# Two gate columns instead of one behind the mixer's last transposes, and one behind its last scan's end

## The chip, the cores and the metric

The kernel runs on one core of one Trainium2 chip. The metric is the device time of one execution in microseconds: a median of 3093.51 us over three runs (3091.14 to 3101.21). TensorE (PE) does the matmuls, VectorE (DVE) and ScalarE (ACT) the elementwise work, and SyncE (SP), ScalarE and GpSimd (POOL) each have a queue from which they issue transfers. Each engine works off its own instructions in the order in which they were built into the program; a wait at the head holds up all that is behind it.

## The reference

A trunk of two layers over 528 tokens (16 learned ones and 512) of width 1024. Each layer is a half-step SwiGLU block, a mixer and another half-step block, each followed by a layer norm of the scaled input plus the block's output. The mixer is what the change touches:

```python
z = x @ w_in
glu_a, glu_b, zr, gate_c, gate_r = split(z)
yc = conv_branch(glu_a, glu_b, ...)      # 31-tap depthwise convolution, layer norm, @ conv_wo
yr = rwkv_branch(zr, ...)                # per head: a state S (64 x 64), stepped through the tokens:
#   S = S * w_t + (S @ -kk_t) (kk_t * a_t)^T + v_t k_t^T ;  y_t = S @ r_t
#   y = group norm of y over each head, + bonus, * g, then @ rwkv_wo
h = sigmoid(gate_c) * yc + sigmoid(gate_r) * yr
return h @ w_out
```

Everything is float32; a product is formed from three matmuls on parts, `hi*xh + hi*xl + lo*xh`, so each weight is split into a high and a low part.

## The kernel before

**The mixer's stages.** A mixer projects the input (the columns of `w_in`, 128 output channels each), runs four scans, each for a quarter of the heads, and then joins the branches. A *column* is one such projection: 8 slices of the input, 3 products and 2 halves of the tokens, 48 matmuls of 264 tokens (L229). 32 columns per layer, 16 for the convolution's gated input and 16 for the two gates, depend on no scan. They are kept in a list, `fill`, and handed out at chosen places by `filler(n)`: so many between the chunks of each scan (`FILL`), so many at each seam between two scans (`FILLS`). They are the last in the list that this change concerns: all of them are gate columns. Such a column is evacuated by a tanh on ScalarE (L1045) and written to memory by ScalarE's queue (L1047).

**A scan.** It goes through 8 chunks of 64 tokens. A chunk is a chain over engines: v transposed (L1349), products with the state (L1354), a copy on ScalarE (L1356), two interleaved product groups (L1363, L1366), a copy (L1369), products that give the output and the state's step (L1371), and two operations on VectorE that make the next state (L1376, L1377). The matmuls of the columns stand in between.

**The end of a mixer.** After a scan its outputs are group normed on VectorE (L1408 to L1429), transposed (L1470), scaled (L1472 on ScalarE), given the bonus and the gate (L1474, L1475 on VectorE) and written to `yscr` (L1476; in the last scan by POOL's queue). The last scan's first half is treated during its second half; its second half after its end. The join then reads `yscr` back (L1537, POOL), casts it to a high part (`rh`, L105) and a low part (`rl`, L106), and multiplies by `rwkv_wo` (L210). The convolution's result is read from `cscr` (L1549, SP) for its layer norm.

**What sets the order.** The program is written out by a scheduler that orders each engine's instructions by the order of the code and by when their inputs are expected, so a column whose weights are there may be placed earlier than where the code calls for it, and some L229 matmuls of one column stand apart from the rest. `nosync(later, earlier)` adds an order that the scheduler must keep, with no wait on the chip. `self.later` uses it: the next column's first matmul is kept behind the named instruction. `self.turned` is the last transpose (L1470).

**A column's weights.** SP loads the raw weights (two buffers). For gate columns ScalarE casts the high part in two halves (L140), writes the negated raw into the low part (L146), and a transfer on POOL's queue adds (L147). The high and low parts have two buffers each, so a column's parts can be made only when the column two before it is finished. The first two columns of `rwkv_wo` use the same buffers, in one cast (L142) and a subtraction on VectorE (L153).

Of the kernel before, what the change touches and what calls it, by code (L numbers as in the profile page):

```python
# [70 lines left out]

FILL0 = (0, 0, 0, 0, 2, 0, 0, 0, 2)
FILL = ((0, 0, 0, 0, 0, 0, 0, 0), (0, 0, 0, 0, 0, 0, 0, 0), (0, 0, 0, 0, 0, 0, 0, 0), (0, 1, 0, 1, 0, 1, 0, 0))
FILLS = (3, 3, 4, 2)
FILLP = ((0, 0, 0, 0, 0, 0), (0, 0, 0, 0, 0, 2), (0, 0, 0, 0, 0, 1), (0, 0, 0, 0, 0, 0))
LAST = 1
SCORES = (2, 1, 1, 1, 1, 1, 1, 1)


# [12 lines left out]
class Trunk:  # L92
# [645 lines left out]
    def mixer(self, l, last, pre, more):  # L738
# [48 lines left out]
        def filler(n):  # L787
            for _ in range(min(n, len(fill))):
                fill.pop(0)()
# [3 lines left out]
        def prep(q):  # L793
            Q = {}
            for i, _ in enumerate(self.prep(q, Q)):
                filler(FILLP[q][i])
                self.taps(TAPP[q])
            return Q
# [14 lines left out]
        for q in range(4):  # L813
# [27 lines left out]
            post = early or self.post(q, Q)  # L841
            filler(FILLS[q])
            Q, N = N, prep(q + 2) if q < 2 else None
        for _ in post:
            pass
        filler(len(fill) - LAST)
        self.later = self.turned
        filler(len(fill))
# [485 lines left out]
    def scan(self, q, Q):  # L1334


        nc, mp = self.nc, self.mp
        G, SB, pc, sv = Q["G"], self.sb, Q["pc"], Q["sv"]
        hc = lambda x: x.rearrange("p (h v) -> p h v", h=4)
        ysb = mp.tile([P, NCH * 4, 32], F32, name="b4", bufs=B4)  # L1340
        ysb = ysb.rearrange("p a b -> p (a b)").rearrange("p (m h v) -> p m h v", m=4, h=4)
        Q["y"] = ysb
        for c in range(NCH):
            cs = slice(NM + c * C, NM + (c + 1) * C)
            left = lambda h: slice(h * HS, (h + 1) * HS)
            right = lambda h: slice(256 + h * HS, 256 + (h + 1) * HS)
            tr = self.sm("tr")
            for p in range(2):
                nc.tensor.transpose(tr[0:C, p * P:(p + 1) * P], Q["v"][p][:, cs], self.ident)  # L1349
            nc.scalar.copy(sv[0:C], hc(tr[0:C, 0:256]))  # L1350
            va, w = (mp.tile([P, 4, HS], F32, name=x, bufs=n) for x, n in (("va", 2), ("w0", W0)))
            nc.scalar.copy(va[0:C], hc(tr[0:C, 0:256]))
            for h in range(4):
                nc.tensor.matmul(tr[0:C, right(h)], G[:, h // 2, h % 2, 0, cs], sv[:, h, :],  # L1354
                                 start=True, stop=True)
            nc.scalar.copy(w[0:C], hc(tr[0:C, 256:512]))  # L1356


            ch = self.sm("ch")
            chain = []  # L1360
            rows = slice(0, P if c + 1 < NCH else C)
            for h in range(4):
                chain.append(nc.tensor.matmul(ch[C:P, left(h)], G[0:C, h // 2, h % 2, 1, cs],  # L1363
                                              w[0:C, h, :], start=h == 0, stop=True,
                                              skip_group_check=True))
                chain.append(nc.tensor.matmul(ch[0:C, right(h)], G[HS:P, h // 2, h % 2, 1, cs],  # L1366
                                              sv[HS:P, h, :], start=h == 0, stop=False,
                                              skip_group_check=True))
            nc.scalar.copy(va[C:P], hc(ch[C:P, 0:256]))  # L1369
            for h in range(4):  # L1370
                chain.append(nc.tensor.matmul(ch[rows, right(h)], SB[:, c, h, rows], va[:, h, :],  # L1371
                                              start=False, stop=True, skip_group_check=True))
            nsv = None
            if c + 1 < NCH:
                nsv = self.new_state()
                nc.vector.tensor_tensor(nsv[HS:P], hc(ch[HS:P, 256:512]), sv[HS:P], op=ALU.add)  # L1376
                nc.vector.tensor_tensor(nsv[HS:P], nsv[HS:P],  # L1377
                                        pc[HS:P, :, c + 1:c + 2].to_broadcast([HS, 4, HS]),
                                        op=ALU.mult)
            for later, earlier in zip(chain[1:], chain):  # L1380
                self.nosync(later, earlier)
            ro = C * (c % 2)
            nc.scalar.copy(ysb[ro:ro + C, c // 2], hc(ch[0:C, 256:512]))
            sv = nsv
            yield
# [305 lines left out]
```

## Time and profile before

| | |
|---|---|
| median of three runs | 3093.51 us (3091.14 to 3101.21) |
| the profiled execution's own time | 3093.63 us, span 3091.9 us |
| TensorE busy | 2972.3 us, 96% of the span |
| VectorE, ScalarE, GpSimd busy | 2278.3, 1436.2, 178.3 us |
| chain that ended last, by engine | TensorE 82%, VectorE 7%, DMA 5%, ScalarE 3% |
| column matmuls (L229) | 5280, about 300 ns each as shown |
| end of the last scan to the join's first product, layer 0 | 1020.72 to 1041.12 us |
| the same, layer 1 | 2544.09 to 2563.67 us |

A matmul's duration as shown overlaps the next one's, so the pace is read from starts, not from durations. The clock that TensorE was granted is given per stretch as a share of its full speed; it is 1.00 or 0.50 at any moment. Idle time stands in brackets in front of the instruction that waited, with what released it. Line numbers are those of the kernel before; in the changed kernel lines after 845 are one higher, and after 1382 two higher.

### The profile page before, as it was taken

How to read it: one execution, taken by the hardware profiler on the slowest of the kernel's cores; microseconds unless marked ns; L12 is line 12 of the kernel's file. 1: busy time of each engine (PE TensorE's matmuls, PEld its weight loads, DVE VectorE, ACT ScalarE, POOL GpSimd, SP SyncE). 2: the span in 40 equal slices, each digit the busy share in tenths (PEclk: the TensorE clock that was granted, in tenths of full speed). 3: DMA queues.
4: the chain of work that ended last, by engine and by line, in shares of the span. 5: the costliest groups of instructions: out<-in, count | busy, mean ns of one | idle time of the engine just before them, and what ended most of it. 6: DMA issues, size and time to landing. Idle time of an engine off the chain costs nothing.

```text
span 3091.9 us, 63773 instructions
## 1 busy us (share of the span) xinstructions
PE 2972.3 (96%) x25908; PEld 2860.6 (93%) x25908; DVE 2278.3 (74%) x4687; ACT 1436.2 (46%) x2551; POOL 178.3 (6%) x286
## 2 busy tenths in 40 slices
PE   8999989999999899999999999899999989999997
PEld 7999989889888899999989999899899879999997
DVE  5676777888876678666786767778888857687767
ACT  4454454344454544444454444543444545254443
POOL 0010000000000000010000000000000000001100
PEclk9999999999999899999999999999899999999998
DMA  6565534335355654565545654344354655546651
GB/s 180 145 148 130 127 108 153 98 86 133 100 125 130 181 147 125 134 149 139 133 121 130 154 130 120 129 147 101 81 127 111 151 129 166 156 121 146 152 139 62
DMA packets 555699, 405.25 MB, mean 131 GB/s; under 512 B 89292, under 2 KB 500288, under 8 KB 555406
## 3 DMA queue, kind: packets, MB, share of 16 engines
q1 hardware_dynamic: 519854, 308.49, 34.8%
q0 software_dynamic: 30944, 84.18, 14.7%
q10 hardware_dynamic: 4608, 8.52, 0.8%
q8 instruction: 203, 3.33, 0.5%
q14 instruction: 90, 0.74, 0.1%
HBM read 270.81 MB, written 47.12 MB: 103 GB/s over the span
## 4 chain that ended last, share of the span: by engine, by line
PE 82%; DVE 7%; DMA 5%; ACT 3%; issue 2%; SPq 1%; ACTq 0%; DVEq 0%; POOLq 0%
PE mm L210 53%; PE mm L229 16%; PE sc L1285 2%; PE ch L1371 2%; PE tr L1354 1%; PE sc L1204 1%; PE ch L1363 1%; DMA w_raw<-in_ffn_wu_dram 1%; DMA w_raw<-in_w_in_dram 1%; DVE cacc L1033 1%; DVE w_lo L153 1%; ACT w_hi L142 1%; PE sc L957 1%; DVE ln_rstd L403 1%; PE sc L1089 1%
## 5 line engine op out<-in xcount | busy, mean ns | idle before, releaser
L210 PE MATMUL mm<-xh,w_hi 128*128 128x264 f32 (+1 forms) x1792 | 515.4, 289 | 20.8 <-ACT xh L417 14.7
L210 PE MATMUL mm<-xh,w_lo 128*128 128x264 f32 (+1 forms) x1792 | 513.9, 287 | 0.5 <-DVE w_lo L153 0.5
L210 PE MATMUL mm<-xl,w_hi 128*128 128x264 f32 (+1 forms) x1792 | 513.8, 287 | 0.5 <-DVE xl L418 0.3
L210 PE MATMUL mm<-hh,w_hi 128*128 128x264 f32 (+1 forms) x1408 | 399.5, 284 | 2.0 <-ACT hh L105 2.0
L210 PE MATMUL mm<-hl,w_hi 128*128 128x264 f32 (+1 forms) x1408 | 399.4, 284 | 0.5 <-DVE hl L106 0.4
L210 PE MATMUL mm<-hh,w_lo 128*128 128x264 f32 (+1 forms) x1408 | 399.7, 284 | 0.0
L229 PE MATMUL mm<-xh,w_lo 128*128 128x264 f32 x1760 | 392.3, 300 | 7.3 <-DMA w_lo<-w_raw 7.0
L229 PE MATMUL mm<-xh,w_hi 128*128 128x264 f32 x1760 | 388.1, 298 | 6.2 <-DVE kp L907 2.9
L229 PE MATMUL mm<-xl,w_hi 128*128 128x264 f32 x1760 | 387.4, 297 | 0.0
L210 PEld LDWEIGHTS mm<-xh,w_hi 128*128 128x128 f32 x1792 | 342.7, 192 | 23.9 <-ACT xh L417 16.6
L1033 DVE SCALAR_TENSOR_TENSOR cacc<-cu,cw,cacc 128x528 f32<-128x528 f32 (+1 forms) x480 | 356.0, 753 | 4.4 <-ACT cacc L1031 0.6
L210 PEld LDWEIGHTS mm<-xl,w_hi 128*128 128x128 f32 x1792 | 344.5, 192 | 1.2 <-DVE xl L418 1.1
L210 PEld LDWEIGHTS mm<-xh,w_lo 128*128 128x128 f32 x1792 | 344.2, 192 | 0.9 <-DVE w_lo L153 0.8
L115 ACT CAST w_hi<-sums 128x512 fp32r<-128x512 f32 (+1 forms) x204 | 154.7, 759 | 318.7 <-PE mm L210 206.7
L229 PEld LDWEIGHTS mm<-xh,w_lo 128*128 128x128 f32 x1760 | 287.4, 196 | 15.1 <-DMA w_lo<-w_raw 8.4
L229 PEld LDWEIGHTS mm<-xh,w_hi 128*128 128x128 f32 x1760 | 287.0, 196 | 12.7 <-DVE kp L907 3.2
L229 PEld LDWEIGHTS mm<-xl,w_hi 128*128 128x128 f32 x1760 | 286.5, 195 | 5.5
L210 PEld LDWEIGHTS mm<-hh,w_hi 128*128 128x128 f32 x1408 | 264.6, 188 | 2.9 <-ACT hh L105 2.4
L210 PEld LDWEIGHTS mm<-hl,w_hi 128*128 128x128 f32 x1408 | 265.0, 188 | 1.2 <-DVE hl L106 1.1
L210 PEld LDWEIGHTS mm<-hh,w_lo 128*128 128x128 f32 x1408 | 265.5, 189 | 0.1
L153 DVE TENSOR_TENSOR w_lo<-w_raw,w_hi 128x1024 fp32r<-128x1024 f32 (+1 forms) x192 | 204.2, 1065 | 82.5 <-ACT w_hi L142 73.3
L142 ACT CAST w_hi<-w_raw 128x1024 fp32r<-128x1024 f32 x136 | 142.3, 1048 | 249.0 <-PE mm L229 84.1
(354 smaller groups left out, 6745.3 us busy)
## 6 DMA issues: line engine op xcount, KB each, us to landing
w_raw<-in_w_in_dram SPq DMA_DIRECT2D x116, 512.0 KB
w_lo<-w_raw POOLq DMA_DIRECT2D x100, 512.0 KB, 5.2
w_raw<-in_ffn_wg_dram SPq DMA_DIRECT2D x88, 512.0 KB
w_raw<-in_ffn_wu_dram SPq DMA_DIRECT2D x88, 512.0 KB
w_raw<-in_ffn_wd_dram SPq DMA_DIRECT2D x80, 512.0 KB
w_lo<-w_raw POOLq DMA_DIRECT2D x68, 256.0 KB, 3.7
w_raw<-in_rwkv_wo_dram SPq DMA_DIRECT2D x16, 512.0 KB
w_raw<-in_conv_wo_dram SPq DMA_DIRECT2D x16, 512.0 KB
```

Source lines behind the costliest of these rows:

```text
L115: self.nc.scalar.copy(hi, x)
L142: copy = self.nc.scalar.copy(hi[:, :kt], raw[:, :kt])
L153: sub = self.nc.vector.tensor_tensor(lo[:, k], raw[:, k], hi[:, k].bitcast(F32), op=ALU.subtract)
L210: self.nc.tensor.matmul(pm, a[:, k, :], b[:, xk + k, s], start=first and k == 0 and j == 0, stop=last and k == nk - 1 and j == 2, skip_gro ...
L229: m = nc.tensor.matmul(pm[:, h, :n], a[:, wk + k, :], b[:, xk + k, s:s + n], start=first and k == 0 and j == 0, stop=last and k == nk - 1 ...
L403: nc.vector.reciprocal(rstd[:, :n], rstd[:, :n])
L957: nc.tensor.matmul(pm, w[a][r, o, :], x[b][r, s], start=j == 0, stop=j == 2)
L1033: tap = nc.vector.scalar_tensor_tensor(y, x, w, y, op0=ALU.mult, op1=ALU.add)
L1089: nc.tensor.matmul(tr[:, 32 * j:32 * j + 32], sq[:, k0:k0 + P], self.bones[:, ::4], start=True, stop=True)
L1204: pairs.append(nc.tensor.matmul(ps[:, e, p * P:(p + 1) * P], FB[p][r, fs], G[r, p, 1, :, cs], start=True, stop=True))
L1285: nc.tensor.matmul(ps[r, i, cs], vt[r, i], x[r, i, cs], start=True, stop=True)
L1371: chain.append(nc.tensor.matmul(ch[rows, right(h)], SB[:, c, h, rows], va[:, h, :], start=False, stop=True, skip_group_check=True))
```

## The change

At the seam behind the third scan three columns are handed out instead of four. All later columns thus move one place on in the list, and at the end three columns are left instead of two. Before, the first of these two was free to be placed anywhere and the second was kept behind the last transposes. Now the first of three is kept behind the last product of the last scan (L1371 of its last chunk, remembered as `self.scanned`), and the other two behind the last transposes.

```diff
-FILLS = (3, 3, 4, 2)
+FILLS = (3, 3, 3, 2)
...
-LAST = 1
+LAST = 2
...
         for _ in post:
             pass
+        self.later = self.scanned
         filler(len(fill) - LAST)
         self.later = self.turned
         filler(len(fill))
...
             for later, earlier in zip(chain[1:], chain):
                 self.nosync(later, earlier)
+            self.scanned = chain[-1]
```

What the scheduler makes of it is seen in the engines' orders. First TensorE in the last scan of layer 0, from the seventh chunk's last product on (`sc`, `tr` and `ch` are PSUM tiles; `mm` is a column). Before:

```order
L1371 MATMUL ch<-va,sb 128x64 x4
L1349 MATMUL tr<-ident,v 64x128 x2
L229 MATMUL mm<-xh,w_hi 128x264 x2
L229 MATMUL mm<-xl,w_hi 128x264 x2
L229 MATMUL mm<-xh,w_lo 128x264 x2
L229 MATMUL mm<-xh,w_hi 128x264 x2
L229 MATMUL mm<-xl,w_hi 128x264 x2
L1354 MATMUL tr<-sv,G 64x64 x4
L229 MATMUL mm<-xh,w_lo 128x264 x2
L229 MATMUL mm<-xh,w_hi 128x264 x2
L1363 MATMUL ch<-w_12046,G 64x64
L1366 MATMUL ch<-sv,G 64x64
```

Now:

```order
L1372 MATMUL ch<-va,sb 128x64 x4
L1350 MATMUL tr<-ident,v 64x128 x2
L1355 MATMUL tr<-sv,G 64x64 x4
L1364 MATMUL ch<-w_11986,G 64x64
L1367 MATMUL ch<-sv,G 64x64
```

No column matmul stands in the last four chunks any more, in either layer; between the seam's inversion (L1285) and the scan's last product there were 109 in layer 0, and there are 14. Behind the scan's last product stands one whole column, then the last transposes, then two whole columns; before, the transposes came first and one column followed.

Second, POOL's queue at the same end in layer 0 (`G` holds the last scan's scaled outputs). Before:

```order
L1476 DMA yscr_4650<-G 128x272 x2
L147 DMA w_lo<-w_raw 128x1024
L1476 DMA yscr_4650<-G 128x256 x2
L1537 DMA h<-yscr_4650 128x3x528 x2
L1537 DMA h<-yscr_4650 128x2x528
```

Now:

```order
L1478 DMA yscr_4650<-G 128x272 x2
L1478 DMA yscr_4650<-G 128x256 x2
L147 DMA w_lo<-w_raw 128x1024
L1539 DMA h<-yscr_4650 128x3x528 x2
L1539 DMA h<-yscr_4650 128x2x528
```

The transfer for the last column's low weights now stands behind the last two writes of `yscr`, in both layers.

Third, ScalarE from the last scan's last output copy (L1383) to the cast of `rh`. Before:

```order
L1383 COPY b_11429<-ch 64x256
L1045 ACTIVATE glus<-mm 128x528
L1047 DMA gscr_4653<-glus 128x528
L1424 ACTIVATE b_12197<-b_11429 128x512
L1472 ACTIVATE G<-tr,vec 128x256
L1472 ACTIVATE G<-ch,vec 128x256
L142 CAST w_hi<-w_raw 128x1024
L1045 ACTIVATE glus<-mm 128x528
L1047 DMA gscr_4653<-glus 128x528
L394 ACT_TABLE_LOAD
L394 ACTIVATE ln_rstd<-eps 128x1 x2
L105 CAST rh<-h 128x528 x8
```

Now, up to where the first `rwkv_wo` weights are cast:

```order
L1385 COPY b_11369<-ch 64x256
L1426 ACTIVATE b_12137<-b_11369 128x512
L140 CAST w_hi<-w_raw 128x512
L1046 ACTIVATE glus<-mm 128x528
L1474 ACTIVATE G<-tr,vec 128x256
L1474 ACTIVATE G<-ch,vec 128x256
L1048 DMA gscr_4653<-glus 128x528
L140 CAST w_hi<-w_raw 128x512
L146 ACTIVATE w_lo<-w_raw 128x1024
L142 CAST w_hi<-w_raw 128x1024
L1046 ACTIVATE glus<-mm 128x528
L1048 DMA gscr_4653<-glus 128x528
```

The last column's two casts, its negated copy and one more gate now stand around the scaling of the last transposes; the rows that follow are the same as before from the second `L142` on.

## The prediction

> **What bounds the kernel now.** I read the groups of waits of TensorE first, then TensorE's own order of time at the end of both mixers, then the other engines there. The two longest waits that a mixer's end can own are these (columns: total us, times, longest):
>
> ```profile
> PE tr L1470 <- DVE b L1429: 14.8, 2, 7.7
> PE mm L210 <- ACT rh L105: 7.8, 2, 3.9
> ```
>
> Both occur once a layer. TensorE's order of time shows them in place; first layer 0, then layer 1 (start, duration, in brackets the idle time before):
>
> ```profile
> 1020.04 0.68 PE L1371 MATMUL ch<-va,sb 128*64 128x64 f32 x8
> 1028.42 0.66 PE L1470 MATMUL tr<-ident,b 128*128 128x128 f32 x2 [7.70 <-DVE b L1429]
> 1029.15 0.79 PE L229 MATMUL mm<-xh,w_hi 128*128 128x264 f32 x2
> 1036.81 0.41 PE L229 MATMUL mm<-xh,w_lo 128*128 128x264 f32 x2
> 1041.12 1.03 PE L210 MATMUL mm<-rh,w_hi 128*128 128x264 f32 x3 [3.90 <-ACT rh L105]
> ...
> 2543.41 0.68 PE L1371 MATMUL ch<-va,sb 128*64 128x64 f32 x8 [0.67 <-ACT va L1369]
> 2551.14 0.66 PE L1470 MATMUL tr<-ident,b 128*128 128x128 f32 x2 [7.05 <-DVE b L1429]
> 2563.67 0.58 PE L210 MATMUL mm<-rh,w_hi 128*128 128x256 f32 x1 [3.89 <-ACT rh L105]
> ```
>
> The scan's last product ends at 1020.72 (2544.09). TensorE idles 7.70 us (7.05) while VectorE normalises the last two chunk pairs, does the last transposes, works off the one held column, and idles 3.9 us more until the join's first product. From the transposes to that product it is 12.70 us (1041.12 less 1028.42), in layer 1 12.53 us. The same stretch by windows (length, busy of PE, PEld, DVE, ACT, POOL, then granted clock):
>
> ```profile
> 996.00:1020.70 24.70, 24.62 (x250) 22.04 (x248) 13.76 (x52) 16.52 (x37) 2.88 (x4) 1.00 0.66 176
> 1028.40:1033.60 5.20, 5.18 (x24) 5.20 (x25) 1.61 (x4) 1.02 (x2) 2.00 (x4) 0.50 0.15 53
> 1033.60:1037.10 3.50, 3.50 (x30) 3.40 (x28) 0.00 (x0) 0.09 (x1) 1.32 (x2) 1.00 0.86 263
> ```
>
> After the idle time the clock is half for 5.2 us, 0.217 us a matmul (5.2 over 24); then 30 matmuls take 3.5 us, 0.117 each. A column is 48 matmuls: 5.6 us warm, and 8.1 us as it ran here (1029.15 to 1037.22).
>
> **The change part by part.** No arithmetic is added or removed. By the order of the built programs, what leaves the last scan's tail is two columns: between the seam's inversion and the scan's end the layer-0 program had 109 column matmuls and has 14, and the last four chunks have none. One column goes behind the scan's last product, two go behind the last transposes. So a layer has three terms.
>
> **Term 1, the scan's tail.** The chunk step is a chain over engines, and its first product (L1354) marks its beat:
>
> ```profile
> 978.18 0.65 PE L1354 MATMUL tr<-sv,G 128*64 128x64 f32 x8
> 982.83 0.30 PE L1354 MATMUL tr<-sv,G 128*64 128x64 f32 x2
> ...
> 1000.35 0.68 PE L1354 MATMUL tr<-sv,G 128*64 128x64 f32 x8
> 1006.28 0.68 PE L1354 MATMUL tr<-sv,G 128*64 128x64 f32 x8
> 1017.49 0.65 PE L1354 MATMUL tr<-sv,G 128*64 128x64 f32 x8
> 2186.89 0.75 PE L1354 MATMUL tr<-sv,G 128*64 128x64 f32 x8 [1.47 <-DVE sv L1377]
> 2190.54 1.97 PE L1371 MATMUL ch<-va,sb 128*128 128x64 f32 x8
> 2194.42 1.08 PE L1354 MATMUL tr<-sv,G 128*64 128x64 f32 x8 [1.19 <-DVE sv L1377]
> ```
>
> The shortest step, with hardly a column matmul in its way, took 4.65 us. The last four of layer 0 run from 1000.35 to 1020.72, 20.37 us: steps of 5.7 on average (17.14 over three) and 3.2 for the last. From 2186.89 on the steps had no column to work on, only two score products, and one took 7.53 us; the windows over it:
>
> ```profile
> 952.00:956.00 4.00, 4.00 (x22) 3.86 (x21) 3.86 (x6) 0.00 (x0) 0.00 (x0) 0.62 0.70 178
> 2186.90:2194.40 7.50, 6.33 (x44) 4.76 (x45) 4.63 (x9) 2.47 (x7) 0.00 (x0) 0.53 0.04 9
> 2194.40:2204.00 9.60, 9.58 (x57) 7.85 (x57) 6.60 (x13) 2.48 (x7) 0.00 (x0) 0.50 0.27 71
> ```
>
> Steps without columns ran at half clock. A bare step of the new tail has the gated multiply (0.42) between the two state operations at most:
>
> ```profile
> 1016.47 0.42 DVE L1475 TENSOR_TENSOR yf<-yf,gg 128x256 f32<-128x256 f32 x1
> 2189.36 0.37 ACT L1369 COPY va<-ch 64x256 f32<-64x256 f32 x1 [0.69 <-PE ch L1366]
> 2193.07 0.75 DVE L1033 SCALAR_TENSOR_TENSOR cacc<-cu,cw,cacc 128x512 f32<-128x512 f32 x1
> ```
>
> At full clock that is 4.65 and 0.42, 5.1 us. At half clock it is 7.53 less what stood in the chain there: 0.81 (va ready at 2189.73, L1371 at 2190.54) and the 0.75 of L1033, with 0.42 added: 6.4 us. Full clock throughout: three steps of 5.1 and 3.2, 18.5 us, 1.9 saved. Half clock after the first step: 5.1, twice 6.4 and a last part of 4.2 (its two large products longer by 0.4 and 0.4, the rest by 0.2), 22.1 us, 1.7 lost. The tail may start earlier by 0 to 2.0 us (17 column matmuls fewer after the seam's transposes); I take 0.7, since the copies behind these transposes remain. Together between 2.6 saved and 1.0 lost; I take 0, nearer the half clock that such steps had. So 11 us of products leave a stretch in which TensorE was 24.62 of 24.70 us busy, and it hardly gets shorter: the steps beneath last nearly as long.
>
> The Trainium skill, page "TensorE: Matmul & The Clock Gate", section "Why this matters for your kernels", says that the clock drops after gaps of more than about 3 us without a matmul. The half-clock rows above have no idle time over 1.47 us, so this trace does not bear it out for such steps; the result by that rule is the second rival.
>
> **Term 2, from the scan's end to the transposes.** The first held column stands ahead of the transposes on TensorE. Starting cold it takes 8.1 us as the held column did (5.6 if warm, 10.4 if cold throughout). The normalisation beneath needs 7.05 us as in layer 1; the 7.70 of layer 0 hold most of a weight split that now comes later:
>
> ```profile
> 1020.99 1.23 DVE L153 TENSOR_TENSOR w_lo<-w_raw,w_hi 128x1024 fp32r<-128x1024 f32 x1 [3.64 <-ACT w_hi L142]
> ```
>
> The gap of 7.70 (7.05) becomes 8.1: 0.4 (1.05) us later. The idle time is filled, but the column hides nothing that was due sooner.
>
> **Term 3, from the transposes to the first product.** Here a queue is passed. The third column's low weights come by an accumulating transfer on POOL (L147). It stood ahead of the last two writes of yscr; now it stands behind them, and they need the transposes, ScalarE and VectorE. Its weights also take the place of the first held column's, so ScalarE can cast only once that column is done:
>
> ```profile
> 1009.38 0.61 ACT L140 CAST w_hi<-w_raw 128x512 fp32r<-128x512 f32 x1
> 1021.37 0.61 ACT L1045 ACTIVATE glus<-mm 128x528 f32<-128x528 f32 x1
> 1029.11 0.56 ACT L1472 ACTIVATE G<-tr,vec 128x256 f32<-128x256 f32 x1 [4.71 <-PE tr L1470]
> 1037.01 1.04 ACT L142 CAST w_hi<-w_raw 128x1024 fp32r<-128x1024 f32 x1 [6.88 <-PE mm L229]
> 1040.45 1.68 ACT L105 CAST rh<-h 128x528 fp32r<-128x528 f32 x3
> ...
> 1013.61 0.88 POOL L147 DMA_DIRECT2D w_lo<-w_raw  x1 [3.69 <-ACT w L1356]
> 1031.69 0.54 POOL L1476 DMA_DIRECT2D yscr<-G  x1 [0.24 <-DVE G L1475]
> DMA to landing us min/median/max: 4.6/5.1/6.4
> ```
>
> Counted from the transposes: the second yscr write was issued by 3.8 us (1031.69 and 0.54, less 1028.42). Now half a cast and the gate's tanh (0.6 each) precede L1472, which so starts at 1.25 instead of 0.69: 4.4 us. L147 lands 5.1 later (4.6 to 6.4), at 9.5 (9.0 to 10.8). The second column occupies TensorE from 0.7 to 6.3; the third does the 4 matmuls that need no low weights, until 6.8, and waits 2.7 us. Its other 44 take 5.1 warm, 7.5 if the wait halves the clock for 5.2 us (24 and 20 matmuls). A wait of 2.29 did so:
>
> ```profile
> 948.47 0.44 PE L1278 MATMUL sc<-dd,ut 64*64 64x64 f32 x2 [2.29 <-DMA dd<-xdscr]
> ```
>
> with 0.62 granted after it, but another of 1.01 lay close before; I take the middle, an end at 15.8. Then the chain from a column's end to the join's first product is as before, 3.9 us: ScalarE casts the second weight, evacuates the gate, loads its table and casts rh, in that order, from 1037.01 to 1040.45. So 19.7 us instead of 12.70 (12.53): 7.0 (7.2) later. Three things are queued behind. The reads of yscr on POOL come after L147, about 1.2 us later than now, under the columns. The raw weights of the join's second column take the buffer that L147 reads, so SP issues their load at 9.5 instead of long before; a load of that size took 5.56 us, which ends at 15.1, just ahead of the cast that wants it. And the conv branch's load on SP waits for the last gate's write, so it moves with that column's end and gives nothing back:
>
> ```profile
> 745.13 5.56 DMA w_raw<-in_w_in_dram
> 1038.60 0.33 ACTq L1047 DMA_DIRECT2D gscr<-glus  x1
> 1042.09 1.45 SPq L1549 DMA_DIRECT2D a<-cscr  x3
> ```
>
>
> **The sum.** Layer 0: 0 and 0.4 and 7.0, 7.4 us. Layer 1: 0 and 1.05 and 7.2, 8.2 us. Together 15.6 us on the profiled execution's own 3093.63 us (span 3091.9, 1.7 around it), whose difference from the median of 3093.51 is nothing: **3109 us**. Its own range is 3099 to 3119: with all lower bounds 2.0 and 2.9 us a layer, with all upper ones 15 and 16, which is unlikely at once.
>
> **The rivals.** First, on the other side: the tail is bound by TensorE's issue, as its 24.62 of 24.70 us busy say, so the 95 columns' matmuls that leave shorten it by 11.1 us, dense bare steps keep the clock up, the gap is 7.0 and the third column warm (9.5, 5.1 and 3.9: 18.5 after the transposes). Then a layer gains 6.0 (5.1) and the time is 3082.5. It decides once a bare step is below 3.6 us; against it stands the fastest step of 4.65.
>
> Second, the clock stays full although steps are bare: 2.6 saved in the tail, the gap 7.0, 18.5 after the transposes: 2.5 and 3.4 later, 3099.5. For it speaks that the drop at 2186.89 came only after several thin steps.
>
> Third, the changed queue place costs nothing because the transfer is early enough, so the columns run back to back: 0.7, 5.6, 5.6 and 3.9, 15.8; 3.5 and 4.3 later, 3101.5. Against it: L147 cannot be issued before the yscr writes.
>
> **How the numbers follow.** About 0.3%, 9.3 us, is what can be told from no change. The forecast has 0.55, the first rival 0.13, the second 0.22, the third 0.10. Slower by over 0.3% (above 3102.8) gets nearly all of the forecast and parts of the last two, 0.58; within 0.3%, most of the second and third and the near end of the first, 0.31; faster, the rest of the first, 0.11. The range 3088 to 3121 leaves the first rival's centre out below and the upper bounds above.
>
> **What would show it.** Right: the wait of 14.8 us on L1429 is nearly gone; the wait for rh stays at 3.9 a layer; a new wait of 2 to 3 us on w_lo stands in the third column; granted clock near 0.5 over the last three chunk steps, 6 us and more each; the first join product 18 to 21 us after the transposes. Wrong: steps below 4.5 us, a clock of 1.00 there, or the third column without a wait.

## The result: 0.84% slower, where 0.50% was forecast

The changed kernel took 3125.60 us (median of five runs, 3109.58 to 3128.82), the kernel before, run beside it, 3093.51 us (3084.44 to 3103.66). The ratio is 1.0084, 95% interval 1.0058 to 1.0110: slower by 26 us, between 18 and 34. The direction was the forecast one. The median lies 4.6 us above my range's upper end; by the ratio the time is 3119.5, just inside. My sum was 15.6 us, and the profiled execution grew by 32.0 us (span 3123.9 us, mean clock 0.961, after 3091.9 and 0.969). So the sum holds about half of what the profiled execution lost, and 60% of what the ratio gives.

**The waits.** TensorE's waits in groups, changed kernel (total us, times, longest):

```profile
PE mm L210 <- ACT rh L105: 12.5, 2, 7.7
PE mm L229 <- DMA w_lo<-w_raw: 10.8, 7, 3.2
PE tr L1355 <- DVE sv L1378: 8.1, 10, 1.5
PE ch L1364 <- ACT w L1357: 4.4, 10, 0.5
```

and the rows of before that answer to the last three:

```profile
PE mm L229 <- DMA w_lo<-w_raw: 7.0, 6, 2.9
PE tr L1354 <- DVE sv L1377: 4.3, 7, 1.5
PE ch L1363 <- ACT w L1356: 1.6, 4, 0.5
```

The 14.8 us in front of the last transposes are gone, as meant. But the waits inside the scan grew by 3.8 and 2.8 us, the wait for low weights by 3.8, and the wait for `rh`, which I had expected to stay at 3.9 a layer, by 4.7.

**TensorE in order of time**, first layer 0, then layer 1 (start, duration, in brackets the idle time before):

```profile
1020.77 1.12 PE L1372 MATMUL ch<-va,sb 128*64 128x64 f32 x8 [0.47 <-ACT va L1370]
1021.82 0.81 PE L229 MATMUL mm<-xh,w_hi 128*128 128x264 f32 x2
1030.14 0.38 PE L1472 MATMUL tr<-ident,b 128*128 128x128 f32 x2
1039.47 0.51 PE L229 MATMUL mm<-xh,w_lo 128*128 128x264 f32 x2 [2.37 <-DMA w_lo<-w_raw]
1046.23 0.40 PE L229 MATMUL mm<-xh,w_lo 128*128 128x264 f32 x2
1054.29 1.03 PE L210 MATMUL mm<-rh,w_hi 128*128 128x264 f32 x3 [7.65 <-ACT rh L105]
...
2566.72 1.12 PE L1372 MATMUL ch<-va,sb 128*64 128x64 f32 x8 [0.47 <-ACT va L1370]
2574.67 0.38 PE L1472 MATMUL tr<-ident,b 128*128 128x128 f32 x2
2584.37 0.81 PE L229 MATMUL mm<-xh,w_lo 128*128 128x264 f32 x2 [2.77 <-DMA w_lo<-w_raw]
2592.27 0.41 PE L229 MATMUL mm<-xh,w_lo 128*128 128x264 f32 x2
2597.51 1.01 PE L210 MATMUL mm<-rh,w_hi 128*128 128x256 f32 x3 [4.84 <-ACT rh L105]
```

The first held column fills the gap ahead of the transposes, 1021.89 to 1030.14. The third column stands still for 2.37 (2.77) us. From the transposes to the join's first product it is 24.15 us (22.84), before 12.70 (12.53).

**By windows**, the last four chunk steps of each layer, changed kernel (length, busy of PE, PEld, DVE, ACT, POOL, granted clock, DMA share, GB/s):

```profile
996.60:1021.89 25.29, 20.16 (x148) 16.28 (x148) 10.74 (x40) 9.75 (x24) 2.01 (x3) 0.50 0.36 96
2543.39:2567.83 24.44, 19.32 (x145) 15.89 (x145) 6.92 (x17) 8.45 (x22) 1.15 (x2) 0.50 0.20 62
```

and before:

```profile
1000.35:1020.72 20.37, 20.29 (x215) 18.01 (x214) 9.71 (x35) 12.99 (x29) 2.88 (x4) 1.00 0.68 176
2524.98:2544.09 19.11, 18.25 (x201) 16.23 (x200) 7.89 (x17) 12.70 (x28) 2.02 (x3) 1.00 0.59 164
```

67 and 56 matmul records fewer stand in these steps, and yet they take 4.92 and 5.33 us more, at a clock of 0.50 from end to end instead of 1.00.

**The account.** Over both layers: the last four steps 10.25 us longer, the gap 0.34 (8.25 and 6.84 after 7.70 and 7.05), the stretch from the transposes to the first product 21.76. Together 32.35 us; what lies elsewhere adds up to nothing in these two profiles (earlier by 3.8 us ahead of the last four steps of layer 0, later by 5.2 in layer 1, earlier by 2 after the last join began). That it does so is partly luck: in the profiles of the kernels below, what lies outside the three stages is between 12 us less and 14 us more than in the kernel before.

**What the stretch behind the transposes waits for** is in the chain of waits of the changed kernel (start, duration, what):

```profile
1034.29 5.14 DMA w_lo<-w_raw
1039.43 0.02 SPq L131
1039.48 10.62 DMA w_raw<-in_rwkv_wo_dram
1050.18 0.04 ACT w_hi L142
...
2579.11 5.21 DMA w_lo<-w_raw
2584.38 8.97 DMA w_raw<-in_rwkv_wo_dram
```

The accumulating transfer lands; only then does SP issue the raw weights of the join's second column, which share the buffer; and that load took 10.62 and 8.97 us. I had given it the 5.56 us of a load beside which no other queue moved data. ScalarE's cast (L142) came 3.54 us behind the third column's end (1046.64), and behind the cast, in ScalarE's order, stand the gate, the table and `rh`.

### The profile page after: what moved, and what is told of

It is laid out like the page before. It is cut to its first block, busy times and chain, and to the rows that moved or that the text cites. A ratio compares the mean times of both kernels' runs of the same rounds, so it can differ in the third digit from the quotient of the medians.

```text
span 3123.9 us, 63780 instructions
## 1 busy us (share of the span) xinstructions
PE 2991.4 (96%) x25908; PEld 2874.1 (92%) x25908; DVE 2279.5 (73%) x4687; ACT 1435.6 (46%) x2551; POOL 178.5 (6%) x286
## 4 chain that ended last, share of the span: by engine, by line
PE 80%; DVE 7%; DMA 6%; ACT 3%; issue 2%; SPq 1%; ACTq 0%; POOL 0%; DVEq 0%; POOLq 0%
PE mm L210 51%; PE mm L229 15%; PE ch L1372 2%; PE sc L1286 2%; PE tr L1355 1%; PE sc L1205 1%; PE ch L1364 1%; DMA w_lo<-w_raw 1%; DMA w_raw<-in_w_in_dram 1%; DMA w_raw<-in_ffn_wu_dram 1%; DVE w_lo L153 1%; DMA w_raw<-in_rwkv_wo_dram 1%; PE sc L958 1%; DVE ln_rstd L403 1%; ACT w_hi L142 1%
## 5 line engine op out<-in xcount | busy, mean ns | idle before, releaser
L210 PEld LDWEIGHTS mm<-xh,w_hi 128*128 128x128 f32 x1792 | 342.4, 192 | 23.6 <-ACT xh L417 16.8
L229 PEld LDWEIGHTS mm<-xh,w_hi 128*128 128x128 f32 x1760 | 285.8, 195 | 12.7 <-DVE kp L908 3.2
L142 ACT CAST w_hi<-w_raw 128x1024 fp32r<-128x1024 f32 x136 | 142.3, 1048 | 263.1 <-PE mm L229 75.8
```

Of the source, the lines that this page charges most:

```text
L142: copy = self.nc.scalar.copy(hi[:, :kt], raw[:, :kt])
L210: self.nc.tensor.matmul(pm, a[:, k, :], b[:, xk + k, s], start=first and k == 0 and j == 0, stop=last and k == nk - 1 and j == 2, skip_gro ...
L229: m = nc.tensor.matmul(pm[:, h, :n], a[:, wk + k, :], b[:, xk + k, s:s + n], start=first and k == 0 and j == 0, stop=last and k == nk - 1 ...
```

## The experiments

My theory after the result had two parts. **Part A**: behind the transposes the last column's weights are late, and the join's raw weights behind them later still. **Part B**: the bare tail halves the clock, and this costs some 5 us a layer. Rivals: the seam with one column fewer costs by itself; POOL's queue place makes the transfer late; the join waits for the reads of `yscr`; the bare steps are as long at any clock.

The edits below are against the changed kernel unless the text names another. The stages are read from TensorE's order of time (first state product of the fifth chunk, end of the scan's last product, transposes, first join product), layer 0 / layer 1. The last column but one is the sum of the three stages over both layers against before (79.46 us); the last is the measured ratio, in us of 3093.51 with its interval.

| kernel | last four steps | gap | transposes to product | stages, us | measured, us |
|---|---|---|---|---|---|
| before | 20.37 / 19.11 | 7.70 / 7.05 | 12.70 / 12.53 | 0 | 0 |
| changed | 25.29 / 24.44 | 8.25 / 6.84 | 24.15 / 22.84 | +32.4 | +26 (18 to 34) |
| seam alone | 20.11 / 20.05 | 7.77 / 6.79 | 11.63 / 12.21 | -0.9 | -5 (-12 to 1) |
| one behind each, four at the seam | 21.69 / 20.34 | 7.07 / 7.81 | 12.52 / 12.42 | +2.4 | 0 (-6 to 6) |
| low weights by VectorE | 25.22 / 23.04 | 7.08 / 7.76 | 18.91 / 17.82 | +20.4 | +12 (7 to 18) |
| `yscr` writes by SP | 25.24 / 24.44 | 6.89 / 6.93 | 23.67 / 22.51 | +30.2 | +24 (15 to 33) |
| own raw buffer | 25.30 / 24.35 | 7.54 / 8.22 | 19.76 / 21.28 | +27.0 | +19 (12 to 26) |
| VectorE and own gate tile | 25.23 / 24.44 | 7.22 / 6.96 | 16.18 / 16.24 | +16.8 | +14 (9 to 19) |
| spare matmuls, 12 a step | 28.02 / 28.36 | 6.80 / 6.79 | 22.75 / 22.70 | +36.0 | +37 (29 to 45) |
| spare matmuls, 8 a step | 22.68 / 22.99 | 6.80 / 6.80 | 22.63 / 22.23 | +24.7 | +26 (18 to 33) |
| one free, one behind each | 21.74 / 22.32 | 7.61 / 7.52 | 12.73 / 12.08 | +4.5 | -4 (-9 to 2) |
| seam, table behind `rh` | 20.14 / 19.27 | 7.78 / 6.79 | 11.70 / 10.39 | -3.4 | +5 (-1 to 11) |

The stage sums come from one execution each, the ratios from five rounds; they agree within the intervals or some 3 us beside them, so the stages named carry the loss.

### The seam alone

```diff
-        self.later = self.scanned
+        self.later = None
...
-LAST = 2
+LAST = 1
```

> Only the seam is changed: three columns at the third seam, and the column that is left over goes where the scheduler wants it (one column stays behind the last transposes, as before). By the built order the last scan's tail keeps its columns (110 and 78 column matmuls behind the inversion, before 109 and 84). Theory A (the loss lies behind the last scan and in its bare tail): the last scan's end, the gap and the join are as before, and the time is within 6 us of the kernel before, some 25 us under the changed one. Theory B (the seam that is one column short leaves the inversion's chain bare and halves the clock at the start of the last scan, as layer 1 of the changed kernel showed between 2498 and 2512 us): half or more of the loss is here already, 12 us over the kernel before.

The ratio is 0.9983 (0.9961 to 1.0004), and every stage at the end is as before to about 1 us. One column fewer at the seam costs nothing that shows (by the interval at most 1 us); theory B is out. What costs is where the columns that are left go.

### One column behind the scan, one behind the transposes

```diff
-FILLS = (3, 3, 3, 2)
-LAST = 2
+FILLS = (3, 3, 4, 2)
+LAST = 1
```

> Four columns at the third seam as before; the first of the two columns left is kept behind the last scan's last product, the other behind the last transposes. The last three chunk steps are bare, one column less stands at the end than in the changed kernel, and the last column's transfer is not late, since the column two before it is finished early. Theory A (the end of the changed kernel is long because the last column's low weights and the join's raw weights come late): the one column behind the transposes starts warm and ends after 5.6 us, the join's first product comes 9.5 to 10.5 us after the transposes (before 12.7, changed 24), the bare tail takes 2 to 4 us of that back, and the time is within 6 us of the kernel before. Theory B (what costs is the column ahead of the transposes and the bare tail): 8 to 15 us over the kernel before.

1.0001 (0.9981 to 1.0021), as theory A has it. But the join's first product did not come at 9.5 to 10.5 us: 12.52 and 12.42. The column had ended 6.5 us after the transposes (which began at 1025.37), and yet (ScalarE and TensorE in order of time):

```profile
1034.88 0.30 ACT L394 ACTIVATE ln_rstd<-eps 128x1 f32<-128x1 f32 x2
1037.20 1.70 ACT L105 CAST rh<-h 128x528 fp32r<-128x528 f32 x3 [2.03 <-issue]
1037.88 1.03 PE L210 MATMUL mm<-rh,w_hi 128*128 128x264 f32 x3 [6.04 <-ACT rh L105]
```

ScalarE was done with all that stands ahead of `rh` at 1035.18 and waited 2.03 us more. The view names no releaser there. But the first of the three reads of `yscr`, issued at 1030.37, took 6.8 us to landing, until about 1037.2, when the cast starts; and in the kernel with one column free, further down, the view puts the same wait down to that read. In the kernel before, the first read landed 9.2 us after the transposes (issued at 1032.70, 4.9 us to landing), and the column with its 3.9 us chain ended later than that and set the product. Here the read landed 11.8 us after them, and it, not the column, sets the product. Why it took longer is not shown. So one warm column behind the transposes hides under this way through memory, and two do not (16.2 us at best, as a later run shows). I had looked at the chain of the columns only.

This kernel also shows what a bare step costs at each clock, over its last four steps:

```profile
996.61:1007.38 10.77, 9.41 (x99) 7.93 (x99) 7.99 (x31) 8.05 (x19) 2.00 (x3) 0.99 0.80 202
1007.38:1018.30 10.92, 8.39 (x69) 6.92 (x69) 1.70 (x4) 4.11 (x10) 0.88 (x1) 0.50 0.58 142
2528.85:2538.73 9.88, 7.45 (x85) 6.19 (x85) 5.10 (x12) 7.25 (x18) 1.15 (x2) 1.00 0.59 181
2538.73:2549.20 10.47, 7.96 (x69) 6.54 (x69) 1.70 (x4) 3.66 (x9) 0.88 (x1) 0.55 0.52 127
```

The sixth chunk's step, the first without columns, took 4.97 and 4.88 us at full clock; the seventh 6.67 and 6.22, with 0.50 and 0.55 granted over the last two. So the clock fell about one bare step after the columns ended.

### Low weights by VectorE

```diff
-DMACOLS = tuple(range(42, 58))
+DMACOLS = tuple(x for x in range(42, 58) if x != 49)
```

> The changed kernel, but the last column's low weights are formed by VectorE (two subtractions in place of ScalarE's negated copy and the accumulating transfer). The raw weights' buffer is then free some 7 us sooner, so the join's second load can start sooner. Theory A (late low weights, and behind them the late raw load, make the third column and the join late): the wait of 2.4 us in the third column and the 3.8 us that ScalarE waits for raw weights are gone, the column runs warm, the join's first product comes 15 to 17 us after the transposes instead of 24, and the time falls by 12 to 18 us, to 8 to 14 us over the kernel before. Theory B (the join waits for the reads of yscr, or the clock sets the pace): the first product moves by less than 3 us and the time by less than 6 us.

Ratio 1.0040 (1.0022 to 1.0057): about 14 us of the 26 are gone, in theory A's 12 to 18. The wait in the third column is gone, and it ended 12.3 us after the transposes. The product came later than I expected all the same, at 18.91 (17.82), because a wait that had been hidden is now seen (ScalarE, then TensorE):

```profile
1042.99 0.61 ACT L1046 ACTIVATE glus<-mm 128x528 f32<-128x528 f32 x1 [2.64 <-DMA gscr<-glus]
1046.15 1.03 PE L210 MATMUL mm<-rh,w_hi 128*128 128x264 f32 x3 [6.63 <-ACT rh L105]
```

The third gate's evacuation waits until the second gate's write has left the one tile that both use.

### The `yscr` writes by SP

```diff
-YQ = (3,)
+YQ = ()
```

> The changed kernel, but the last scan's writes of yscr are issued by SP instead of POOL, so that the last column's accumulating transfer (L147) no longer stands behind two of them. Theory A (ScalarE's negated copy, which in layer 0 of the changed kernel ended at 1033.61, sets L147, and the queue place only the 0.7 us until 1034.29): L147 is issued 3.3 to 3.8 us after the transposes instead of 4.15, the third column still waits 1.5 to 2.4 us, the join's first product stays 22 to 24.5 us after the transposes, and the time is within 4 us of the changed kernel's. Theory B (as my forecast had it, the place in POOL's queue is what makes the low weights late): the third column waits no longer, the join's first product comes 16 to 20 us after the transposes, and the time falls by 8 to 16 us.

Ratio 1.0078 (1.0049 to 1.0107), the stages as in the changed kernel: theory A. POOL, ScalarE and TensorE in layer 0, where the transposes began at 1031.26:

```profile
1033.66 1.07 ACT L146 ACTIVATE w_lo<-w_raw 128x1024 fp32r<-128x1024 f32 x1
1035.02 0.86 POOL L147 DMA_DIRECT2D w_lo<-w_raw  x1 [33.52 <-ACT w_lo L146]
1040.23 0.81 PE L229 MATMUL mm<-xh,w_lo 128*128 128x264 f32 x2 [2.04 <-DMA w_lo<-w_raw]
```

With nothing ahead of it on POOL, the transfer starts 3.76 us after the transposes instead of 4.15, because ScalarE's negated copy ends only then, and the third column still waits 2.04 us. The queue place that I made the cause costs 0.4 us (0.7 in layer 1, 3.75 after 4.44). What makes the weights late, by the order of the waits, is the two-deep ring of weight buffers: ScalarE's first cast for them (L140) waits for the first held column to end, in the changed kernel until 1030.09. No run has a third buffer, so this is read and not tested.

### The last column's raw weights in a buffer of their own

```diff
+raw = self.mp.tile([P, 2 * T], F32, name="FB", bufs=2) if own else ...
...
-        return self.wunit(w[:, :, col * P:(col + 1) * P], dma=col in DMACOLS)
+        return self.wunit(w[:, :, col * P:(col + 1) * P], dma=col in DMACOLS, own=col == 49)
```

> The changed kernel, but the last gate column's raw weights are loaded into memory that is free by then (a tile of the third scan's factors), so the join's second load of raw weights no longer waits for the last column's transfer. Theory A (that load, issued only when L147 lands and then 10.7 us long instead of the 5.56 I took, holds ScalarE's cast 3.7 us behind the third column): the cast follows the third column at once, the join's first product comes 19.5 to 21 us after the transposes instead of 24.15 and 22.85, the wait for low weights in the third column stays, and the time falls by 5 to 9 us. Theory B (the cast of rh waits for the reads of yscr at that point anyway): the first product moves by less than 1 us.

Ratio 1.0062 (1.0040 to 1.0083), some 7 us less. The chain of waits now goes from the low weights straight through the column to the cast:

```profile
1032.52 4.57 DMA w_lo<-FB
1037.13 6.93 PE mm L229 x42
1044.08 0.02 ACT w_hi L142
```

The product comes 19.76 us after the transposes in layer 0: the load had cost 4.4 us there. In layer 1 it is 21.28; there the load had held the cast only 0.7 us behind the column, and the column itself was slow.

### VectorE, and a tile of its own for the last gate

```diff
-        s = self.tmp("glus", 1)
+        s = self.tmp("kp" if o == 15 else "glus", 1)
```

(on the kernel with low weights by VectorE)

> The kernel with the last column's low weights from VectorE, and besides its gate is evacuated into a tile of its own, so that it no longer waits for the landing of the previous gate's write (2.64 us in layer 0 of that run, where the third column ended 12.3 us after the transposes and the join's first product came at 18.91). Theory A (of the 11 us that the two columns behind the transposes cost in the changed kernel, late weights, the late raw load and then this wait are all that is avoidable; what is left is two warm columns and the 3.9 us from a column's end to the product): first product 15.8 to 16.8 us after the transposes, 2 to 6 us less time than without the new tile, so 6 to 11 us over the kernel before. Theory B (the join waits for the reads of yscr, some 12.4 us after the transposes and later where transfers crowd): it stays above 17.5.

16.18 and 16.24 us in both layers, theory A; here the two columns run warm and nothing on the way waits for a transfer. That is 12.3 us for two columns and the 3.9 us chain (ScalarE in layer 0, from the cast behind the third column to the table):

```profile
1047.11 1.04 ACT L142 CAST w_hi<-w_raw 128x1024 fp32r<-128x1024 f32 x1 [4.28 <-PE mm L229]
1048.06 0.60 ACT L1046 ACTIVATE kp<-mm 128x528 f32<-128x528 f32 x1
1049.05 1.28 ACT L394 ACT_TABLE_LOAD   x1 [0.39 <-ACT kp L1046]
```

So of the changed kernel's 24.15 and 22.84 us, 16.2 are two columns and the chain, and 7.97 and 6.60 are late weights and what followed from them. The total did not show the last 4 us: 1.0045 (1.0028 to 1.0062), not told apart from 1.0040. With the tail still bare it stays 14 us over the kernel before.

### Spare matmuls in the tail

```diff
+        def keep(tr, after):
+            xh = self.x[0]
+            for i in range(NWARM):
+                m = nc.tensor.matmul(tr[C:P, 0:P], xh[:, i, 0:C].bitcast(F32), xh[:, i, 0:P].bitcast(F32),
+                                     start=True, stop=True)
+                self.nosync(m, after)
+                after = m
+            return after
...
+            warm = q == 3 and c >= WARM
+            d0 = keep(tr, m) if warm else None
```

> The changed kernel with spare matmuls that nobody reads (three groups of four 128x128 products a chunk step, in the last four chunks, in rows of the same PSUM tile that are otherwise unused): one group where TensorE waits for the state, one where it waits for w, one where it waits for va. Theory A (the steps of the tail are long because their thin work halves the granted clock): the clock stays at or comes back to 1.00 in the tail, its steps take 4.7 to 5.6 us instead of 6.6 to 7.8, and a layer is 2 to 5 us shorter. Theory B (the chain over ScalarE and VectorE sets the step whatever the clock): the steps stay at 6.5 us or more, with a clock of 1.00. Theory C (the clock stays at 0.50 even when TensorE is dense there): the steps get longer by 0.5 to 1.5 us and the time by 4 to 10 us.

Theory A's clock came, its steps did not: 1.00 in the last two steps of layer 0, but 7.16 us for the seventh. The experiment was badly built. ScalarE's copy of `w` waited for the spare matmuls too, since they write the same tile:

```profile
1002.50 0.82 PE L1350 MATMUL tr<-xh 128*64 128x128 f32 x6
1003.35 0.36 ACT L1374 COPY w<-tr 64x256 f32<-64x256 f32 x1 [1.46 <-PE tr L1350]
```

It tells only that TensorE's density brings the clock back, and that work put on the chain costs more than the clock gives.

### Fewer of them, off the chain

```diff
+            d0 = keep(tr[C:P], m, 2) if warm else None
...
+            d1 = keep(ch[0:C], m, 4) if warm else None
...
+                d2 = keep(tr[C:P], chain[-1], 2)
```

> The changed kernel with spare matmuls in the last four chunk steps again, but fewer (8 products of 128x128 a step) and placed so that no copy of the chain has to wait for them: two while the state is formed, four while w is copied (into an unused part of the tile that the next group writes anyway), two while va is copied. In the run before, each of three groups of four took about 1.05 us and the copies waited for two of them. Theory A (half the clock makes a bare step 6.6 us; at full clock it is 5.0 to 5.8): the clock is 1.00 from the second bare step on, the steps take 5.0 to 5.8 us, the last four 20 to 22 us instead of 25.3 and 24.4, and a layer is 3 to 5 us shorter. Theory B (the chain takes 6.6 us at any clock): 6.4 us or more at 1.00. Theory C (so little work doesn't bring the clock back): 0.50, and steps of 6.6 to 7.3 us.

The last two steps of each layer, with spare matmuls:

```profile
1008.19:1017.26 9.07, 8.08 (x97) 6.76 (x97) 3.17 (x8) 3.64 (x10) 1.12 (x2) 1.00 0.19 62
2566.28:2575.36 9.08, 8.09 (x97) 6.76 (x97) 1.70 (x4) 3.12 (x9) 0.00 (x0) 1.00 0.09 31
```

Clock 1.00, steps of 5.79 and 3.28 us, where the changed kernel has 6.62 and 4.25 at 0.50: 1.8 us less over two steps, although more matmuls stand in them (97 records, 69 there). With the bare steps of 4.97 and 6.67 us above, at full and at half clock, this shows that a good part of a bare step's length is the clock: theory B is out, C too. The last four steps took 22.68 and 22.99, a little over A's 20 to 22, since the first of them still ran partly at half clock (7.29 and 8.12 us). The ratio of the whole, 1.0083 (1.0059 to 1.0108), doesn't show the gain of nearly 8 us that the stages have against the changed kernel, 4.1 of it in the last four steps. The stage sum, +24.7, is in line with its own ratio, so the clearer witness is that sum; but a gain in the total is not shown.

### One column free, one behind the scan, one behind the transposes

```diff
-        self.later = self.scanned
-        filler(len(fill) - LAST)
+        filler(len(fill) - LAST); self.later = self.scanned; filler(1)
```

> Three columns at the third seam as in the changed kernel, but of the three that are left the first is free, the second is kept behind the last scan's last product and only the third behind the last transposes. Theory A (one column behind the transposes hides under the way of yscr through memory, which takes 12.4 us to the join's first product whether the column starts cold or warm, and two don't; the bare steps are fewer): the last four steps take 20 to 22 us, the gap 6.8 to 7.8, the join's first product comes 11.6 to 12.6 us after the transposes, and the time is between 6 us less and 3 us more than the kernel before. Theory B (the column ahead of the transposes costs by itself): the gap is over 8 us or the join later than 14, and the time 8 us or more over the kernel before.

0.9988 (0.9970 to 1.0005): not told apart from the kernel before. The stages are within about 0.3 us of what theory A said. Here ScalarE's view names what the cast of `rh` waits for:

```profile
1036.80 1.70 ACT L105 CAST rh<-h 128x528 fp32r<-128x528 f32 x3 [2.28 <-DMA h<-yscr]
```

The gap's idle time is used, and nothing is won: the two to three bare steps make the last four 1.4 and 3.2 us longer.

### A candidate: the table load behind the casts of `rh`

```diff
-            nc.scalar.activation(rstd[:, 0:1], eps, AF.Sqrt)
+            t = nc.scalar.activation(rstd[:, 0:1], eps, AF.Sqrt); silu and self.nosync(t, self.parted[0])
```

(on the kernel with the seam alone)

> A candidate, not a test of the forecast: only one column fewer at the third seam (the run that was 0.17% under the kernel before, not distinguishable), and ScalarE's table load and its small activation (1.5 us together), which stand ahead of the casts of rh, put behind them. If the chain from the column's end (cast, gate, table, rh) sets the join's first product, it comes 10 to 10.7 us after the transposes instead of 11.63 and 12.21, and the time is 2 to 4 us lower, about 0.25 to 0.3% under the kernel before. If the reads of yscr set it, at 11.5 to 12.4 us, nothing changes.

First product at 11.70 and 10.39, the ratio 1.0015 (0.9996 to 1.0034). The time from the column's end to the product fell from 3.9 to 2.5 us in both layers, as the chain says; but in layer 0 the column itself ended 9.2 us after the transposes (7.7 with the seam alone), so the product did not move. The total shows no gain. I found no version that beats the kernel before by more than can be measured.

## Why the prediction was right in sign and too small in size

**The frame held.** The wait on L1429 is gone; filling it hid nothing; the loss lies in the two places that I named. Where the sum had 0, 1.45 and 14.2 us over both layers for its three terms, the stages measured 10.25, 0.34 and 21.76. The gap came out at 8.25 us as forecast in layer 0 (8.1), and in layer 1 at 6.84, 1.3 less, with 0.85 granted while the column ran.

**Term 1 was the first mis-sized step.** "I take 0", with a loss of at most 1.0: it was 4.92 and 5.33. The prices of a step were right: 6.4 at half clock (6.62 measured), 5.1 at full (4.88 and 4.97 in the kernel with one column behind each), 4.2 for the last (4.25). The count was not. I let the clock fall only "after the first step"; it was at 0.50 for all four (the first took 6.65 and 6.95). I left the transposes of the scan's first half out: most of them stand in the second step of layer 0, which took 7.77. And I set an earlier start of the tail against it. It came in layer 0, by 3.75 us, but in layer 1 the start was 5.2 us later than the join before it accounts for, with 0.69 granted over the scan's first step (2507.05 to 2514.74) and waits of 1.47 and 1.75 us just ahead of the four. The kernel with the seam alone has the same two, 3.8 us earlier and 5.5 later, and is no slower for it. Having quoted a row in which steps without columns ran at 0.53, I took 0, a value between its price and that of full clock; the row should have been taken as it stood. Without the earlier start, three steps of 6.4 and one of 4.2 are 23.4 us, 3.0 more than before in layer 0. I also let layer 0's 20.37 us stand for both layers; layer 1's tail had taken 19.11, so there the same 23.4 is 4.3 more.

**Term 3 was the second.** 19.7 us forecast, 24.15 and 22.84 measured. Down to the wait it was close: low weights at 9.5 (9.29 and 9.65), wait 2.7 (2.37 and 2.77), the column's end at 15.8 (16.5 in layer 0). In layer 1 the end came at 18.0, as the 44 matmuls took 8.3 us, with 0.64 granted over them, where I had put 5.1 to 7.5. The step that failed is "a load of that size took 5.56 us, which ends at 15.1, just ahead of the cast that wants it": it took 10.62 and 8.97, and the product came 3.75 and 0.93 us later than the column's end and 3.9. I had priced a transfer in a crowded stretch by a row beside which no other queue moved data, with a margin of 0.7 us. The Trainium skill, page "DMA: Bandwidth & Descriptors", section "Queues, rings and completion order", says that each of the sixteen engines goes round between the queues that have work for it, packet by packet; the trace agrees for the time from 1044.5 to 1046.5 (packets, MB, share of the engines):

```profile
q0 software_dynamic: 162, 0.60, 73.8%
q1 hardware_dynamic: 166, 0.08, 14.0%
```

The first is POOL's queue with the three reads of `yscr` (2.1 MB), the second SP's with this load and another of 512 KB. Each has about as many packets as the other, but the loads' are small, and so they get an eighth of the bytes. From 1047 to 1050, with the reads nearly done, SP's queue moved 0.80 MB. From 1039.5 to 1043.5 the trace has no packet of SP's queue beside 254 of POOL's, and that the rule doesn't explain. No run changes the traffic alone, so its part in the 10.62 us is read from the trace and not tested.

**The cause I gave inside term 3 was wrong.** The number fitted by luck, and not since L147 "cannot be issued before the yscr writes": without them ahead of it on POOL it started 0.4 us earlier. The third rival's condition was half true: the queue place costs next to nothing, but the transfer isn't early enough either. ScalarE's work on these weights starts when the first held column ends, and with four instructions around it takes until 3.5 us after the transposes.

**The rivals.** The first (clock up, 6.0 gained) is out: a bare step at full clock is 4.9 us, not below 3.6. The second rested on the clock staying full. The Trainium skill, page "TensorE: Matmul & The Clock Gate", section "Why this matters for your kernels", has the clock drop after gaps of more than about 3 us; in this trace it dropped without one. Half clock lasted from 996.3 to 1026.9 in layer 0, with no idle time of TensorE over 1.11 us in it and none over 1.64 in the 6 us before:

```profile
990.00:996.00 6.00, 3.57 (x44) 2.81 (x41) 5.60 (x19) 4.16 (x8) 0.00 (x0) 1.00 0.42 134
996.30:1026.90 30.60, 25.16 (x170) 21.29 (x171) 14.52 (x53) 11.04 (x27) 2.01 (x3) 0.50 0.30 80
1027.00:1031.00 4.00, 4.00 (x35) 4.00 (x34) 1.36 (x6) 0.91 (x2) 0.00 (x0) 0.99 0.00 0
```

## What to carry to other kernels

Work that covers a chain of small matmuls also holds TensorE's clock up: before taking it away, price the bare chain at half clock from its first step on (here 6.6 us a step against 4.9), and don't take a value in between. A place that waits for a round trip through memory has room for so much work and no more; measure the round trip in the kernel as it will be (the first read landed 9.2 us after the transposes in the kernel before, 11.8 with one column on each side of them) beside the work and its chain (one cold column 12.7 us; two warm ones 16.2). When work is moved behind such a place, follow its buffers to the next load, and price that load by the traffic at that time.

## What had not been expected of the hardware

The granted clock was 0.50 over a stretch in which TensorE was busy, as shown, 20.16 of 25.29 us, with 148 matmul records in it; with spare matmuls, 97 records in 9.07 us, it was 1.00. How much work it takes to hold it up lies between these and is not measured closer. It was full again only from 1027 on, 5.2 us after dense work had begun at 1021.82; in layer 1 it took 2.1 us. The trace's own record of the clock changes in stretches of 3.4 us or multiples of it.

Executions of one kernel differ by this: the candidate's runs lie between 3078.15 and 3108.97 us, and its profiled execution was the shortest of all profiled here,

```profile
core 0: 3076.4 us, clock 0.977
```

with the clock full for more of the time than in any other (0.960 to 0.969). So a gain of some 7 us in the stages can vanish in the ratio of five rounds, and it takes both: the stages, from one execution each, say where time went, and only the ratio says whether the whole got faster.

The accumulating transfers for the low weights (L147) took 4.5 to 7.8 us from issue to landing in the changed kernel, and the one at the end of each layer, 5.14 and 5.21, delayed by as much the load that waited for its source.
